# A hybrid decoder step: query and key chunks of the second mixer as pairs through memory, heads and page attention behind fourteen whole gates

## The chip, the cores and the metric

The kernel runs on one core of a Trainium2 chip. The time is the device time of one execution in microseconds (us), as the median of several runs. Engines are named as the profile names them: PE (TensorE, matmuls), PEld (its weight loads), DVE (VectorE), ACT (ScalarE), POOL (GpSimd) and SP (SyncE, which issues loads).

## The reference

One layer of a hybrid decoder, on 512 prompt tokens and 8 single decode tokens together (N = 520 columns, model width 2048). Cut to what matters:

```
sh1, sc1, g1, sh2, sc2, g2 = ada_mod(c, w_ada, b_ada)          # silu(c) @ w_ada + b_ada, six parts
h = modulate(rmsnorm(x, norm1_w), sh1, sc1)
mq, mk, mv, mo, mi, mf, fq, fk, fv, ff, ga, gb = split(h @ w_in + b_in)
y_m = mlstm(mq, mk, mv, mi, mf, mo)                            # first mixer, 4 heads
q_f = rmsnorm(split_heads(fq, 8), f_qnorm_w)
k_f = rmsnorm(split_heads(fk, 8), f_knorm_w)
y_f = fox(q_f, k_f, v_f, log_sigmoid(ff))                      # second mixer, 8 heads
merged = sigmoid(ga) * (y_m @ w_proj_a) + sigmoid(gb) * (y_f @ w_proj_b)
x = x + g1 * (merged @ w_out)
h2 = modulate(rmsnorm(x, norm2_w), sh2, sc2)
x = x + g2 * conv_ffn(h2, ...)
```

For the prompt, `fox` is causal attention with a forgetting bias. For each of the 8 decode tokens it attends to two pages of 128 cached keys and values, which a page table names, and to the token itself.

## The kernel before

All activations are stored with features on the 128 partitions and the 520 tokens along the free axis. A weight matrix is cut into *chunks* of 128 output features: a chunk of `w_in` is 128 x 2048 numbers, 1 MB. Products are made in a split precision: weights and activations are each divided into a high and a low part (`wh`, `wl` and so on; ACT casts the high part, DVE subtracts for the low one), and high x high, high x low and low x high are added in PSUM.

There are two ways to compute chunks.

- *Dense* (`dense`): for each of 16 k-blocks (K = 2048 in blocks of 128), three products for each of two halves of the tokens (260 columns): 96 matmuls. Half a chunk of weights (128 x 1024) is loaded by SP (`wraw`, a pool of 8 tiles named `raw`) and split (`wtwo`). Between k-blocks `dense` calls `step()`, which runs one entry of the list `bg`; twice a chunk it calls `due()`, which may run an entry of `pending`, by a pattern in `calls`. One k-block is called a *step* here; other work is put at steps by number.
- *In pairs* (`Pair`, `run_pairs`): two chunks are computed together with Strassen's scheme in seven products of half size, each 8 k-blocks x 3 matmuls of 260 columns (168 matmuls for two chunks). The sums of activations that this needs (`hX`) are made once; sums of weights (`sw`) are made by DVE for every pair. `run_pairs` counts in products, seven a pair; `late` maps such a number to a function that runs there. Inside it PE, DVE and ACT keep the order in which the program lists their instructions.

Everywhere else a scheduler orders instructions by their place in the program and a cost model. Loads of weights have priority and leave as soon as a tile is free.

The stages around the change, in order:

1. First mixer with dense chunks, then a few dense gates `ga` while its last heads finish (NG = 2 gates).
2. `w_pa`: 16 dense chunks of `y_m @ w_proj_a`; the conditioning part G1 rides on it as `pending` work.
3. *Pairs*: `GatePair` for the other gates `ga` (2 to 15) and for the first NB2 = 8 gates `gb`, and `ValuePair` for the values of the second mixer, which go to memory (`dv`). Sigmoids of these `gb` gates go to memory as `dsg`.
4. *Attention stage*: for each of the 8 heads a dense chunk of queries and one of keys (`f_proj`, tile `fi`), then the 8 other gates `gb` dense (`w_gate`, tile `gate`). Between their k-blocks run the heads (`f_norm_q`, `f_norm_k`, `f_scores`, `f_turn`, `f_attend`: root mean square norms, scores, softmax, transposes, products with values) and the page attention of the decode tokens (`s_rows`, `s_load` with gathers of key pages by POOL into `kp`, `s_scores` on DVE, `s_softmax`, `s_gather` with gathers of value pages into `vp`, `s_attend` on PE, `s_heads`). All this is placed by `at(chunk, k, ...)`: a head starts every two chunks, 32 steps; page scores run from the eighth head on, then every 6 steps; the first value gathers come while key gathers still run. The conditioning parts SC2 and SH2 are `pending` work here.
5. `w_pb`: 16 dense chunks of `y_f @ w_proj_b`, each multiplied by its gate `mg[j]` and added to the part from memory (`dmg`); then `w_out` in pairs, and the feed-forward part.

A conditioning part (`ada_steps`) is 16 k-blocks of a 32-column product with 2048 columns of `w_ada` (two loads of 0.5 MB a k-block), done as 8 parts of two k-blocks, and a last entry that transposes the result and adds the bias.

## Time and profile before

| | |
|---|---|
| median of 3 runs | 2865.99 us (2864.04 to 2866.9) |
| span of the profiled execution, first to last instruction | 2875.7 us |
| mean granted TensorE clock in it | 0.996 |
| PE busy | 2845.9 us (99%) |
| DVE, ACT, POOL busy | 2165.4 (75%), 1379.1 (48%), 363.6 us (13%) |
| chain that ended last, by engine | PE 89%, issue 4%, DVE 3%, DMA 2%, ACT 2% |
| moved by DMA | 514.23 MB, mean 179 GB/s |

The profiled execution has no time of its own apart from its span, which is 9.7 us above the median of the timed runs. A row of a window view gives the stretch, its length, busy time and number of instructions of PE, PEld, DVE, ACT and POOL, the granted clock, the busy share of the DMA engines and what they moved. A row of the chain of waits gives start, length, what ran, and how many instructions were merged. A row of a group gives line, engine, operation, output <- inputs, shape, count, busy time, mean length of one in ns, and the idle time before.

### The profile page before, as it was taken

Reading aid. Unit: us, or ns where it says so; the run is one execution under the profiler, and the core shown is the slowest. Engines: PE = TensorE matmul, PEld = TensorE weight load, DVE = VectorE, ACT = ScalarE, POOL = GpSimd, SP = SyncE. Lnnn points to the kernel's source line nnn. Section 1 sums busy time; section 2 is a strip of 40 time slices with the busy share of each in tenths; the row PEclk is TensorE's granted clock in tenths of the full one; section 3 lists DMA queues with packets and bytes.
Section 4 is the critical chain, followed back from the end, with each engine's and each line's share of the span. In section 5 each row is a group of like instructions: output and inputs, shape, how many; then the busy total and the mean of one; then the engine's idle time right before and its main releaser. Section 6 shows DMA issues by size and latency. Waiting matters only on the chain.

```text
span 2875.7 us, 58597 instructions
## 1 busy us (share of the span) xinstructions
PE 2845.9 (99%) x23462; PEld 2734.9 (95%) x23462; DVE 2165.4 (75%) x4016; ACT 1379.1 (48%) x2451; POOL 363.6 (13%) x649
## 2 busy tenths in 40 slices
PE   8999999999999999999999999999999999999999
PEld 6899998999998989799999999999999999999999
DVE  5987754677855667368888888888888887787787
ACT  4346643455544554335555544444444445544543
POOL 0001101221101123302111000000000001100100
PEclk9999999999999999999999999999999999999999
DMA  9934458745456676657763444444443437746752
GB/s 340 313 130 142 141 164 300 246 151 170 148 166 222 208 243 231 209 186 230 221 202 104 128 137 144 144 138 151 135 152 114 149 111 201 191 153 186 204 159 89
DMA packets 214298, 514.23 MB, mean 179 GB/s; under 512 B 24512, under 2 KB 77232, under 8 KB 214024
## 3 DMA queue, kind: packets, MB, share of 16 engines
q1 hardware_dynamic: 177232, 416.07, 44.8%
q0 software_dynamic: 36352, 94.18, 10.9%
q8 instruction: 184, 3.01, 0.4%
q14 instruction: 90, 0.74, 0.1%
q10 hardware_dynamic: 440, 0.23, 0.0%
HBM read 440.47 MB, written 66.46 MB: 176 GB/s over the span
## 4 chain that ended last, share of the span: by engine, by line
PE 89%; issue 4%; DVE 3%; DMA 2%; ACT 2%; POOL 0%; SPq 0%; ACTq 0%; POOLq 0%; DVEq 0%
PE x L60 31%; PE y L60 16%; PE z L60 8%; PE fi L221 7%; PE gate L221 4%; PE fo L60 3%; PE pa L221 3%; PE pre L60 3%; PE mo L221 2%; PE adp L417 2%; PE mv L221 2%; PE adp L60 1%; DMA ar<-in_w_ada 1%; PE mq L221 1%; PE mk L221 1%
## 5 line engine op out<-in xcount | busy, mean ns | idle before, releaser
L60 ACT CAST wh<-sw 128x512 fp32r<-128x512 f32 x638 | 365.7, 621 | 246.2 <-PE z L60 74.2
L60 DVE TENSOR_TENSOR wl<-sw,wh 128x512 fp32r<-128x512 f32 x638 | 411.2, 686 | 86.8 <-ACT wh L60 83.9
L60 PE MATMUL x<-bf,wh 128*128 128x260 f32 x2624 | 475.9, 282 | 0.2 <-DVE tg L60 0.2
L60 ACT CAST wh<-raw 128x1024 fp32r<-128x1024 f32 (+2 forms) x350 | 316.7, 917 | 296.3 <-PE x L60 132.8
L60 DVE TENSOR_TENSOR wl<-raw,wh 128x1024 fp32r<-128x1024 f32 (+2 forms) x350 | 365.8, 1056 | 123.0 <-ACT wh L60 110.5
L60 PEld LDWEIGHTS x<-bf,wh 128*128 128x128 f32 x2624 | 403.4, 188 | 0.4 <-issue 0.4
L60 PE MATMUL x<-bf,wl 128*128 128x260 f32 x1312 | 369.8, 282 | 0.0
L176 DVE TENSOR_TENSOR wl<-raw,wh 128x1024 fp32r<-128x1024 f32 (+1 forms) x115 | 139.5, 1213 | 192.4 <-ACT wh L175 178.9
L60 PEld LDWEIGHTS x<-bf,wl 128*128 128x128 f32 x1312 | 246.9, 188 | 0.0
L60 PE MATMUL y<-bf,wh 128*128 128x260 f32 x1312 | 239.3, 283 | 0.0
L175 ACT CAST wh<-raw 128x1024 fp32r<-128x1024 f32 (+1 forms) x115 | 119.5, 1040 | 216.1 <-issue 42.9
L60 DVE TENSOR_TENSOR sw<-raw,raw 128x512 f32<-128x512 f32 x316 | 203.1, 683 | 0.0
L60 PEld LDWEIGHTS y<-bf,wh 128*128 128x128 f32 x1312 | 201.9, 188 | 0.0
L60 PE MATMUL x<-ff,wh 128*128 128x260 f32 x1024 | 186.5, 283 | 0.0
L60 PE MATMUL y<-bf,wl 128*128 128x260 f32 x656 | 185.1, 282 | 0.0
L60 PEld LDWEIGHTS x<-ff,wh 128*128 128x128 f32 x1024 | 157.8, 188 | 0.0
L60 PE MATMUL x<-ff,wl 128*128 128x260 f32 x512 | 144.6, 282 | 0.0
L60 PE MATMUL x<-hf,wh 128*128 128x260 f32 x720 | 131.4, 283 | 0.0
L60 PE MATMUL fo<-fe,wh 128*128 128x260 f32 x768 | 125.6, 284 | 1.6 <-DVE fo L60 1.1
L60 PEld LDWEIGHTS y<-bf,wl 128*128 128x128 f32 x656 | 123.4, 188 | 0.0
L60 PE MATMUL z<-bf,wh 128*128 128x260 f32 x656 | 120.3, 284 | 0.0
L60 PEld LDWEIGHTS x<-hf,wh 128*128 128x128 f32 x720 | 110.7, 188 | 0.0
(641 smaller groups left out, 7586.9 us busy)
## 6 DMA issues: line engine op xcount, KB each, us to landing
raw<-in_w_fi SPq DMA_DIRECT2D x176, 512.0 KB
raw<-in_w_in SPq DMA_DIRECT2D x155, 512.0 KB
ar<-in_w_ada SPq DMA_DIRECT2D x192, 256.0 KB
raw<-in_w_ada SPq DMA_DIRECT2D x96, 512.0 KB
raw<-in_w_fo SPq DMA_DIRECT2D x64, 512.0 KB
raw<-in_w_out SPq DMA_DIRECT2D x32, 512.0 KB
raw<-in_w_fo SPq DMA_DIRECT2D x32, 384.0 KB
dff<-cc POOLq DMA_DIRECT2D x44, 260.0 KB
```

Of the source, the lines that this page charges most:

```text
L60: return lambda *a, **k: self.tc.keep_in_program_order(getattr(self.eng, op)(*a, **k))
L175: S.copy(wh[:, o], t[:, :m])
L176: V.tensor_tensor(wl[:, o], t[:, :m], wh[:, o].bitcast(F32), op=ALU.subtract)
L221: T.matmul(acc[:, z, :HN], a[:, o], b[:, z * HN:(z + 1) * HN], start=(k == 0 and i == 0), stop=(k == K - 1 and i == 2))
L417: ins = T.matmul(ps[32 * g:32 * g + 32, :], cs[:, k, :], w, start=first, stop=last, tile_position=(0, 32 * g))
```

## The change

- *Queries and keys as pairs.* A new `QueryPair` computes the query and key chunk of one head as a pair and stores both in memory (`dqk`). Eight of them follow the four value pairs. `f_proj` goes; `f_load` fetches queries, keys and values of a head from memory by SP.
- *Fewer gates as pairs.* NB2 goes from 8 to 2: six gates `gb` more become dense, 14 in all. Their chunks are stored without sigmoid (`dsg`), and `put_gate` applies it in the `w_pb` loop, where all 16 gates are now fetched, four chunks ahead.
- *SC2 among the pairs.* The part moves from `pending` into `late_steps`: from the third pair on, each pair has one k-block's loads at its product 2 and the matmuls at product 5; the transpose comes in the last pair.
- *Decode rows.* The queries and keys of the 8 decode tokens are read from `dqk` for all heads at once and normed before the attention stage, instead of being copied head by head.
- *A new plan for the attention stage.* It is written in steps (`put`): a head every 24 steps, page scores every 9 steps from step 12, value gathers from step 164, `s_attend` every 6 steps from 174. SH2 is asked for in the pattern `0, 3, 8`, three calls of `due()` in eight.

The diff, cut to its core:

```diff
+        return [on(part, k) for k in range(0, KC, 2)] + [lambda: ada_store(which, box[1])]
...
-    NB2 = 8
+    NB2 = 2
     assert (NG + NB2) % 2 == 0
-    dsg = dram([NB2, P, N], "dsg")
+    dsg = dram([KC, P, N], "dsg")
...
+    dqk = dram([2, FH, P, N], "dqk")
+
+    class QueryPair(ValuePair):
+        def __init__(self, hh):
+            self.hh = hh
+            self.chunks = [25 + 3 * hh, 25 + 3 * hh + 1]
+            Pair.__init__(self, [I["w_in"][i] for i in self.chunks], hX, ORDER, 1)
+
+        def out(self, e):
+            parts = (self.tt[:, :HN], self.tg[:, :HN]) if e == 0 else (self.tg[:, HN:N], self.tt[:, HN:N])
+            for z, t in enumerate(parts):
+                G.dma_start(dqk[e, self.hh][:, z * HN:(z + 1) * HN], t)
+
     gates = list(range(NG, KC + NB2))
     units = [GatePair(gates[2 * i:2 * i + 2]) for i in range(len(gates) // 2)]
-    units[2:2] = [ValuePair((2 * i, 2 * i + 1)) for i in range(FH // 2)]
+    units[2:2] = [ValuePair((2 * i, 2 * i + 1)) for i in range(FH // 2)] + [QueryPair(hh) for hh in range(FH)]
+    late_ada = {}
+
+    def late_load(k):
+        late_ada[k] = [wraw(I["w_ada"][k * P:(k + 1) * P, SC2 * DM + e * 1024:SC2 * DM + (e + 1) * 1024])
+                       for e in range(2)]
+
+    def late_product(k):
+        if k == 0:
+            late_ada["ps"] = mm_ps("adp")
+        raw = late_ada.pop(k)
+        ada_mm(late_ada["ps"], [(k, raw[g // 2][:, g % 2 * 512:(g % 2 + 1) * 512], k == 0, k == KC - 1)
+                                for g in range(4)], False)
+        if k == KC - 1:
+            late_ada["sb"] = ada_out(late_ada.pop("ps"), 4)
+
+    def late_turn():
+        ada_store(SC2, late_ada.pop("sb"))
+
+    late_steps = {7 * (len(units) - 1) + 2: late_turn}
+    for k in range(KC):
+        late_steps.update({7 * (2 + k) + 2: on(late_load, k), 7 * (2 + k) + 5: on(late_product, k)})
...
-    run_pairs(units, 1, {}, 0)
+    run_pairs(units, 1, late_steps, 0)
...
+    rows = pt("rows")
+    for e in range(2):
+        nc.sync.dma_start(rows[:, e * 64:(e + 1) * 64].rearrange("p (h n) -> p h n", h=FH),
+                          dqk[e, :, :, SEQ:N].rearrange("h p n -> p h n"))
+    sq = pt("sq")
+    S.activation(sq[:, :128], rows[:, :128], AF.Square)
+    psb = mm_ps("sms")
+    T.matmul(psb[:, :128], ones, sq[:, :128], start=True, stop=True)
+    sq = rsqrt([(psb[:, :128], 0, 128)], 1.0 / DK, pt("rq"))
+    V.tensor_tensor(rows[:, :128], rows[:, :128], sq[:, :128], op=ALU.mult)
+    for t, e, c, f in ((qS, 0, C_QN, DK ** -0.5), (kS, 1, C_KN, 1.0)):
+        for g in range(2):
+            o = e * 64 + g * 32
+            V.tensor_scalar(t[:, g].rearrange("p b h -> p h b"), rows[:, o:o + 32].rearrange("p (h b) -> p h b", h=4),
+                            col(c), f, op0=ALU.mult, op1=ALU.mult)
+    rows = sq = t = None
...
-    def f_proj(H, i):
-        wi[0] = 25 + 3 * H.i + i
-        acc, t, n = w_in("fi")
-        S.activation(z2(t), acc, AF.Identity, bias=col(C_BIN + n - 1))
-        return t
-
-    pending += ada_steps(SC2) + ada_steps(SH2)
-    calls[:] = 0, 1, 2
+    def f_load(H):
+        H.q, H.k, H.v = (st("fi") for _ in range(3))
+        for t, src in ((H.q, dqk[0]), (H.k, dqk[1]), (H.v, dv)):
+            nc.sync.dma_start(t[:, :N], src[H.i])
+
+    pending += ada_steps(SH2)
+    calls[:] = 0, 3, 8
...
-    def at(chunk, k, f, *a):
-        plan.setdefault(chunk * KC + k, []).append(on(f, *a))
-
+    def put(s, f, *a):
+        plan.setdefault(s, []).append(on(f, *a))
+
+    HP = 24
     heads = []
     for hh in range(FH):
         H = Head()
         H.i, H.p, H.pt = hh, [], {}
         heads.append(H)
-        c = 2 * hh
-        at(c + 1, 6, f_norm_q, H)
-        at(c + 2, 5, f_norm_k, H)
-        at(c + 2, 7, f_forget, H)
-        at(c + 2, 9, f_values, H)
-        at(c + 2, 14, f_scores, H, 0)
-        at(c + 2, 14, f_scores, H, 1)
-        at(c + 3, 0, f_scores, H, 2)
-        at(c + 3, 2, f_scores, H, 3)
-        for k, j in ((8, 0), (9, 1), (10, 2)):
-            at(c + 3, k, f_turn, H, j)
+        b = 8 + hh * HP
+        if hh:
+            put(b - 12, f_load, H)
+        put(b - 3, lambda H=H: f_square(H, H.q))
+        put(b + 3, f_norm_q, H)
+        put(b + 4, lambda H=H: f_square(H, H.k))
+        put(b + 9, f_norm_k, H)
+        put(b + 11, f_forget, H)
+        put(b + 13, f_values, H)
+        for s, i in ((17, 0), (17, 1), (19, 2), (21, 3)):
+            put(b + s, f_scores, H, i)
+        for j in range(3):
+            put(b + 28 + j, f_turn, H, j)
         for j in range(NB):
-            at(c + 3, 12 + j, f_attend, H, j)
-    for e, c in enumerate((7, 15)):
-        at(c, 12, s_rows, e)
-        for i in range(1 + e):
-            at(c + 1, 2 + 9 * i, s_load, e * 8 + i)
-    for i in range(8):
-        at(8 + i, 11 if i % 2 == 0 else 4, s_scores, i)
-        if i < 7:
-            at(8 + i, 14 if i % 2 == 0 else 7, s_load, i + 1)
-        at(16, 12 + 6 * i, s_scores, 8 + i)
-        if i < 6:
-            at(16, 15 + 6 * i, s_load, 10 + i)
-    for i in range(8):
-        at(18, 12 + i, s_gather, i)
-    at(19, 8, s_bias)
-    at(19, 11, s_softmax)
-    at(20, 2, s_weights)
+            put(b + 34 + j, f_attend, H, j)
+    f_load(heads[0])
+    for e in range(2):
+        put(1 + e, s_rows, e)
+    s0, ds = 12, 9
+    for i in range(16):
+        put(s0 + ds * i - (8 if i else 4), s_load, i)
+        put(s0 + ds * i, s_scores, i)
+    put(154, s_bias)
+    put(155, s_softmax)
+    put(162, s_weights)
+    for i in range(4):
+        put(164 + i, s_gather, i)
     for n in range(8):
-        at(20, 6 + 7 * n, s_attend, n)
-        for i in range(n * 4 + 8, min(n * 4 + 12, 32)):
-            at(20, 6 + 7 * n + 1 + i % 4, s_gather, i)
+        t = 174 + 6 * n
+        put(t, s_attend, n)
+        for i in range(n * 4 + 4, min(n * 4 + 8, 32)):
+            put(t - 5 + i % 4, s_gather, i)
         if n % 2:
-            at(20, 6 + 7 * n + 3, s_heads, n // 2)
+            put(t + 3, s_heads, n // 2)
 
     def y_split(hh):
         yf[hh] = split(sp, "s", yf[hh], "yf", SEQ)
 
     for hh in range(FH):
-        at(19, 14 + 7 * hh, y_split, hh)
+        put(max(182 + 4 * hh, 8 + hh * HP + 39), y_split, hh)
...
-    for H in heads:
-        H.v = st("fi")
-        nc.sync.dma_start(H.v[:, :N], dv[H.i])
-        H.q = f_proj(H, 0)
-        f_square(H, H.q)
-        H.k = f_proj(H, 1)
-        f_square(H, H.k)
     H = None
     mg = [None] * KC
-    calls[:] = 0, 0, 1
 
     def fetch_gate(j):
         mg[j] = st("sgm")
         nc.sync.dma_start(mg[j][:, :N], dsg[j])
 
+    def put_gate(j):
+        if j >= NB2:
+            S.activation(mg[j][:, :N], mg[j][:, :N], AF.Sigmoid)
+
     for j in range(NB2, KC):
-        if j == NB2 + 3:
-            calls[:] = 0, 1, 5
-        mg[j] = w_gate(j, 1)
+        i = 1 + 24 + 24 + KC + j
+        acc = dense(I["w_in"][i], h, "gate")
+        t = st("sgm")
+        S.activation(z2(t), acc, AF.Identity, bias=col(C_BIN + i - 1))
+        G.dma_start(dsg[j], t[:, :N])
+    t = None
     flush()
-    fetch_gate(0)
-    fetch_gate(1)
+    order = [j for i in range(8) for j in (i, 8 + i)]
+    for j in order[:4]:
+        fetch_gate(j)
...
-        if n % 2 == 0 and n // 2 + 2 < NB2:
-            fetch_gate(n // 2 + 2)
+        if n + 4 < KC:
+            fetch_gate(order[n + 4])
+        put_gate(j)
```

More of the change, by code (lines that the diff above doesn't have):

```diff
@@ L517, in part, with ada_store @@
                 box.append(ada_out(box[0], 4))
-        def last():
-            t = ada_turn(box[1], 4)
-            c0 = which * 16
-            dst = ada[:, c0:c0 + 16, :].rearrange("p (g j) i -> p j g i", g=4)
-            bias = wide(C_ADA + c0, 16).rearrange("p (g j) i -> p j g i", g=4)
-            for j in range(4):
-                V.tensor_tensor(dst[:, j], t[:, j, :, :9], bias[:, j], op=ALU.add)
-            if which == SC2:
-                ada_add_one(c0, 16, C_N2)
-        return [on(part, k) for k in range(0, KC, 2)] + [last]
+        return [on(part, k) for k in range(0, KC, 2)] + [lambda: ada_store(which, box[1])]
+    def ada_store(which, sb):
+        t = ada_turn(sb, 4)
+        c0 = which * 16
+        dst = ada[:, c0:c0 + 16, :].rearrange("p (g j) i -> p j g i", g=4)
+        bias = wide(C_ADA + c0, 16).rearrange("p (g j) i -> p j g i", g=4)
+        for j in range(4):
+            V.tensor_tensor(dst[:, j], t[:, j, :, :9], bias[:, j], op=ALU.add)
+        if which == SC2:
+            ada_add_one(c0, 16, C_N2)
     SH1, SC1, G1, SH2, SC2, G2 = range(6)
@@ L1439, in f_norm_k @@
         G.dma_start(O["kT"][:, H.i, :], H.k[:, :N])
-        V.tensor_copy(kS[:, H.i // 4, :, H.i % 4], H.k[:, SEQ:N])
         H.kr = split(sp, "s", H.k, "fk", SEQ, G if H.i < FH - 1 else V)
@@ L1446, in f_norm_q @@
         f_norm(H.q, qwc, H)
-        V.tensor_copy(qS[:, H.i // 4, :, H.i % 4], H.q[:, SEQ:N])
         H.qr = split(sp, "s", H.q, "fq", SEQ, G)
@@ L1862, in tile_hybrid_step @@
     units = [WoPair(c) for c in range(0, KC, 2)]
-    order = [j for i in range(8) for j in (i, 8 + i)]
     early = {}
```

## The prediction

> **What bounds the kernel now.** I read the page's busy shares first, then the stages around the change, then the chain for the price of one matmul, then the places where TensorE loses time.
>
> ```profile
> span 2875.7 us, 58597 instructions
> PE 2845.9 (99%) x23462; PEld 2734.9 (95%) x23462; DVE 2165.4 (75%) x4016; ACT 1379.1 (48%) x2451; POOL 363.6 (13%) x649
> ```
>
> TensorE (PE) is busy in all but 30 us. Busy time can hide a loss, though: a stretch shown below is busy throughout with a quarter fewer matmuls, so I count matmuls. Next the stages, whose columns are PE, weight loads, DVE, ACT, POOL (time and instructions), clock, DMA share, GB/s: the pairs, the attention stage (16 query/key chunks, then 8 gates), and the `w_pb` stage.
>
> ```profile
> 536.00:837.00 301.00, 301.00 (x2521) 301.00 (x2520) 233.27 (x398) 156.79 (x311) 44.95 (x85) 1.00 0.50 165
> 837.00:1229.70 392.70, 387.77 (x3065) 343.75 (x3064) 210.97 (x472) 177.28 (x330) 92.37 (x92) 0.99 0.66 220
> 1229.70:1325.00 95.30, 95.30 (x796) 95.25 (x795) 72.61 (x120) 36.46 (x55) 13.35 (x25) 1.00 0.65 203
> ```
>
> The pairs have no idle PE time at 77% DVE. In the chain of waits (start, length, what, matmuls) the same product returns every pair, the same point of a head every two chunks, and a conditioning part (`adp`) has a piece of its own.
>
> ```profile
> 439.42 11.65 PE pa L221 x96
> 452.92 11.65 PE pa L221 x96
> 519.00 17.18 PE pa L221 x144
> 553.40 5.74 PE x L60 x48
> ...
> 814.44 5.74 PE x L60 x48
> 911.03 3.62 PE fi L221 x30
> 945.04 3.62 PE fi L221 x30
> 1657.35 3.12 PE adp L60 x16
> ```
>
> From 553.40 to 814.44 are 13 pairs: 20.08 us each. A pair is 7 products of 8 x 3 matmuls, 168: 119.5 ns a matmul. A dense chunk is 16 x 3 x 2 = 96 matmuls; 17.18 us for 144 is 119.3 ns, the same. Dense or paired, a matmul costs the same; two chunks are 192 of them dense and 168 as a pair. The matmul count is the bound.
>
> **The change part by part.**
>
> *Chunks that change sides.* Two gates came before (NG = 2): the pairs were 22 gates and 8 values, 15 units (301.0 us / 20.08); they become 16 gates, 8 values, 16 queries and keys, 20 units. The dense gates go from 8 to 14, the dense query/key chunks from 16 to none. Out: 16 x 96 - 8 x 168 = 192 matmuls. Back in: 6 x 96 - 3 x 168 = 72. Net 120 matmuls x 119.5 ns = **-14.3 us**, all on the engine that sets the end. The work around the pairs (ACT, DVE and POOL ends of a query pair: those of a value pair, with half its stores) goes where DVE has 23% free: nothing.
>
> *The SC2 part among pairs.* Its matmuls stay the same; only their grouping changes.
>
> ```profile
> 858.91 1.85 PE adp L417 x16
> ```
>
> Eight blocks of 16 (1.85 us; the `pa` rows stand 13.50 apart, 11.65 + 1.85) become 16 blocks of 8. A block's own cost beyond its matmuls is what a chunk with one loses: 11.65 - 96 x 0.1195 = 0.18 us. Eight blocks more: +1.4 us. From below 0; from above the 3.12 us block, an `adp` inside pairs: 8 x (3.12 - 1.85) + 1.4 = +11.6. I take **+1.4**, since most parts inside pairs and all those before are 1.85 and the loads come three products (8.6 us) ahead. Weight tiles: six of eight slots per unit instead of four. On SP's queue today a pair's loads leave in one group, a pair apart:
>
> ```profile
> 706.59 6.80 SPq L161 DMA_DIRECT2D raw<-in_w_in  x4
> 726.72 6.76 SPq L161 DMA_DIRECT2D raw<-in_w_in  x4
> ```
>
> By the order of release (two slots after the third product, one after the fifth, three after the sixth) every load still leaves at least three products before its use. A pair then moves 3 MB in 21 us, 150 GB/s, beside stores: nothing.
>
> *The rows of the decode queries and keys.* Two small loads, one 128-column matmul, a root and six small DVE steps before the attention stage: +0.5 us on PE, bounded by 0 and by the wait for a load that comes late, some 3 us (`adp` above, 3.12 - 1.85, doubled). `vS`, a load of the same kind, left at 663.3, far ahead of its stage, so I take the low side.
>
> ```profile
> L1418 SPq DMA_DIRECT2D vS<-dv x1: 377/377/377, 663.3 to 663.3; - x1
> ```
>
> *The attention stage.* Heads now come every 24 steps (a step is one k of a dense chunk) instead of 32, page scores every 9 steps from the first head on. Does another engine become the bound? Head periods without and with two page scores, then a pair stretch:
>
> ```profile
> 911.00:945.00 34.00, 34.00 (x276) 30.06 (x274) 17.93 (x43) 17.20 (x34) 3.17 (x3) 1.00 0.61 201
> 1011.80:1045.80 34.00, 34.00 (x275) 30.08 (x275) 21.96 (x51) 17.15 (x34) 7.06 (x7) 1.00 0.76 246
> 1344.00:1404.00 60.00, 60.00 (x504) 60.00 (x503) 51.17 (x98) 34.66 (x58) 11.69 (x18) 1.00 0.69 211
> ```
>
> ```profile
> L176 DVE TENSOR_TENSOR wl<-raw,wh 128x1024 fp32r<-128x1024 f32 x48 | 58.8, 1224 | 118.3 <-ACT wh L175 105.2 <-issue 5.5 <-PE nFb L408 3.5
> ```
>
> A head's own PE work is 34.0 - 192 x 0.1195 - 2 x 1.85 = 7.4 us. A new period is 24 x 6 x 0.1195 + 7.4 + 0.86 x 1.85 = 26.2 us of PE. DVE in it: head 17.93 - 4 x 1.224 = 13.0, three splits 3.7, 2.67 page scores at (21.96 - 17.93) / 2 = 2.0 each 5.4; together 22.1 us, 84%. The last row has DVE at 85% with 504 matmuls in 60.00 us, 119 ns: not slowed. ACT is at 62% by the same sum, POOL lower. I take nothing for it; bounds 0 and 10% of the stage. The evictions of the 14 gates replace those of 16 chunks; their sigmoid moves to `w_pb`, and all 16 gates are now fetched there, four chunks (23 us) ahead:
>
> ```profile
> L1231 ACT ACTIVATE sgm<-gate,sv 128x520 f32<-128x520 f32 x7 | 4.9, 693 | 0.6 <-remote 0.4 <-PE gate L221 0.2
> ```
>
> 14 x 0.69 = 10 us beside ACT's 36.46 of 95.30 us: hidden by the dense matmuls; behind a late gate the weight casts would queue, one chunk ahead of PE. The seam to `w_pb` has 5 steps after the last page head instead of 6:
>
> ```profile
> 1226.72 0.50 DVE L1697 TENSOR_TENSOR yfl<-yS,yfh 128x8 fp32r<-128x8 f32 x4
> ```
>
> This ends 2.5 us before `w_pb` begins at 1229.7; a step less (0.72 us) leaves 1.8. The loads of queries and keys add two transfers per head on SP's queue, where weights stand behind them; eight weight slots cover that. The stores of the gates go to POOL's queue ahead of page gathers: 14 issues, covered because a gather is wanted only 8 steps later.
>
> *Bytes.* The stage moved 392.7 us x 220 GB/s = 86 MB. Less 10 chunks (10.5 MB) and SC2 (16.8), plus queries, keys (4.3) and gate stores (3.4): 66 MB. Length: 392.7 - 10 x 11.47 - 8 x 1.85 - stalls = 250 to 263 us; 250 to 265 GB/s.
>
> *The stalls that exist.* PE loses time near the end of the stage without waiting for a semaphore:
>
> ```profile
> PE gate L221 <- issue: 4.0, 9, 0.7
> ```
>
> ```profile
> 994.00:1002.00 8.00, 8.00 (x66) 7.87 (x65) 5.13 (x10) 3.57 (x8) 3.26 (x3) 1.00 1.01 354
> 1140.00:1148.00 8.00, 7.53 (x56) 6.74 (x54) 5.50 (x8) 0.00 (x0) 6.48 (x6) 1.00 0.90 295
> 1148.00:1156.00 8.00, 5.86 (x28) 4.37 (x28) 4.94 (x8) 1.74 (x2) 5.49 (x6) 0.85 0.71 225
> 1156.00:1164.00 8.00, 8.00 (x49) 7.79 (x50) 2.31 (x5) 2.33 (x2) 0.00 (x0) 0.73 0.41 144
> 1188.00:1196.00 8.00, 7.43 (x58) 6.10 (x57) 1.23 (x1) 1.64 (x2) 2.30 (x3) 1.00 1.02 389
> 1204.00:1212.00 8.00, 6.87 (x51) 5.51 (x52) 1.23 (x1) 1.64 (x2) 2.08 (x3) 1.00 0.51 173
> ```
>
> Against 66 matmuls in 8 us (first row) the next three miss 10 + 38 + 17 = 65, 7.8 us, and the last two 8 + 15, 2.8 us: 10.6 us in all. By busy time they would be 0.5 + 2.1 + 0.0 + 0.6 + 1.1 = 4.3 us, and the stall terms below a gain of 0.6 us instead of 5.8; the 1156 row, fully busy with 49, decides for counts. The Trainium skill (Perfetto Trace Analysis, Identifying the Most-Contended Engine) says the same, that matmul occupancy is no good measure since pipelined matmuls overlap. In that row the clock is 0.73. What stands beside the stalls is POOL's queue, in trains of gathers:
>
> ```profile
> 1136.86 0.95 POOL L877 DMA_INDIRECT vp<-in_cache_v,idx  x1 [0.30 <-issue]
> ...
> 1154.06 0.95 POOL L877 DMA_INDIRECT vp<-in_cache_v,idx  x1 [0.30 <-issue]
> 1188.93 0.95 POOL L877 DMA_INDIRECT vp<-in_cache_v,idx  x1 [0.30 <-issue]
> ```
>
> The long stall starts half-way in a train of 14, in which key gathers (every 6 steps) and the first 8 value gathers run together; the short ones end trains of 8. In the new plan the last key load is at step 139 and the first value gather at step 164, so the train of 14 goes: -7.8. The value gathers keep their trains (4 per 6 steps, 4 per 7 now): 2.8 stays. In exchange SH2's parts come in two bursts of three, 15 weight tiles of 0.5 MB in three calls (28 us) beside 4.9 MB of other loads: 12.7 MB, of which 4 MB can lie ready, at the 295 to 389 GB/s of the rows 22 to 30 us. Within 2 us each of just enough: **+2** for both, bounds 0 and 8. Sum of the stalls: **-5.8**.
>
> *Sum.* -14.3 + 1.4 + 0.5 - 5.8 = -18.2 us. It is made against the profiled execution, whose span, 2875.7, is 9.7 us above the median of the runs, 2865.99; the stages are a few per cent of it, so I subtract from the median: 2847.8, **2848 us**.
>
> **The rivals.**
>
> *The stalls only move.* Gathers, gates and parts stand denser, and PE loses about what it lost (10.6 us): -14.3 + 1.9 = 2853.6 us. For it: 220 GB/s become some 260. Against it: the 994 row, 1.01 and 354 GB/s with 66 matmuls.
>
> *The denser attention stage starves PE (slower).* Place: the two bursts (56 us) and the value gathers (50 us). At the rate of 1140 to 1156 (84 of 132 matmuls, 36% lost) that is 38 us, of which 10.6 are there already: 2865.99 - 12.4 + 27 = 2881. It decides from a loss of 12.4 + 10.6 + 5.7 = 28.7 us, 80 us of such stretches. For it: today's stall came at only 225 to 295 GB/s. Against: that took POOL's longest train. The Trainium skill (Runtime: NRT & Kernel Launch, Instruction fetch mechanics) says that an engine's instructions come by DMA too, and that this is mostly hidden; if these are late instructions, more bytes mean more of them, and by that page alone the price would be near none. No row here tells it apart.
>
> *DVE becomes the bound there.* At 84% its queue delays the splits of the weights; half of the 10% bound, 5% of 252 us: 2848 + 13 = 2861. Against: the 85% row.
>
> *The parts among pairs wait for their tiles.* Slots too few; each of 16 products waits 2 us, a load's landing after a late release: 2848 + 32 = 2880. Against: the release order above.
>
> **How the numbers follow.** Forecast 0.50 (own range 2841 to 2853), moved stalls 0.25, starved PE 0.12, DVE 0.08, tiles 0.05. The low end is -12.4 with all stalls and the extra 1.4 gone, -10.6 - 1.4: 2841, set at 2839; the high end leaves out 0.17 and reaches past the DVE case: 2864. A change under 0.2% (5.7 us) can't be told from none: faster 0.50 + 0.25 + 0.03, same 0.08, slower 0.14.
>
> **What would show it.** The pairs last 20 x 20.08 + 17 = 418 us without idle PE; the attention stage 250 to 256; DVE near 84% in its middle; no 8 us with under 50 matmuls; `w_pb` still 119 to 120 ns a matmul. Wrong if `x`, `y`, `z` of the pairs stand more than 119.5 ns apart, if PE waits for DVE's `wl` or for a `raw` load, or if several windows lose a third of their matmuls.

## The result, and the profile after

The changed kernel takes 2909.35 us (median of 4 runs, 2906.55 to 2911.15), the kernel before 2865.6 us (4 runs, 2864.04 to 2866.9): ratio 1.015, 95% interval 1.0136 to 1.0165. It is 44 us slower, where 18 us faster was forecast. The profiled execution has a span of 2909.5 us, which is typical of its runs.

The window view of the changed kernel, in the same three stages and columns as before: pairs, attention stage, `w_pb`.

```profile
538.00:959.60 421.60, 421.60 (x3495) 405.91 (x3494) 309.56 (x528) 209.46 (x418) 55.69 (x105) 1.00 0.57 190
959.60:1264.40 304.80, 271.68 (x1972) 225.48 (x1971) 190.73 (x440) 146.62 (x298) 102.36 (x105) 0.96 0.64 216
1264.40:1356.00 91.60, 91.60 (x767) 91.60 (x766) 68.08 (x113) 43.30 (x68) 11.76 (x22) 1.00 0.71 224
```

The first and the last row are as forecast: no idle PE time, 421.6 us against 418, and 119.4 ns a matmul in `w_pb`. The loss is in the middle row. It was to last 250 to 256 us; it lasts 305, with PE idle for 33 us and the granted clock at 0.96. Its bytes are as counted ahead: 304.8 us at 216 GB/s are 65.8 MB, against 66. Its worst stretch, ten microseconds to a row:

```profile
1020.00:1030.00 10.00, 8.50 (x68) 7.92 (x70) 7.26 (x12) 3.52 (x6) 2.56 (x3) 1.00 0.98 314
1030.00:1040.00 10.00, 5.02 (x36) 1.29 (x35) 5.60 (x10) 3.80 (x7) 1.45 (x2) 1.00 0.91 315
1040.00:1050.00 10.00, 2.73 (x6) 0.38 (x8) 0.00 (x0) 0.00 (x0) 2.57 (x3) 0.51 0.99 372
1050.00:1060.00 10.00, 10.00 (x56) 6.57 (x53) 4.74 (x22) 4.82 (x13) 0.00 (x0) 0.81 0.38 129
```

From 1040 to 1050 almost nothing computes (PE starts 6 matmuls) and the DMA engines are full (0.99, 372 GB/s). The chain of waits says what is awaited:

```profile
970.06 1.85 PE adp L417 x16
...
1032.32 2.77 PE adp L417 x22
...
1035.37 0.54 SPq L161
...
1036.00 13.15 DMA raw<-in_w_ada
1049.15 0.04 issue
1049.19 1.92 PE adp L417 x4
...
1067.27 8.90 DMA fi<-dqk
...
1107.22 4.90 DMA raw<-in_w_ada
1112.16 4.45 PE adp L417 x12
```

A part of SH2 (16 matmuls) that stands alone takes its 1.85 us, like the one at 970.06. By the plan its eight parts come 0, 48, 336, 384, 432, 720, 768 and 816 dense matmuls into the stage. In the trace, counted in PE's order, the scheduler has put parts 4 and 5 and 10 matmuls of part 6 together at 384, with no dense matmul between them, and the other 38 at 672. A weight tile serves 4 of these matmuls, so 42 need 11 tiles, and the pool has 8 slots. The tiles of part 6 could be asked for only from 1035.37 on, when the products before it had given slots free, and the one that the chain names takes 13.15 us to land. PE keeps its order and waits. The 42 matmuls take 22.4 us from start to next start and the 38 take 11.4, where 1.85 us for every 16 would be 4.9 and 4.4.

In the 1050 row the clock is at 0.81 although PE has work again. The Trainium skill (TensorE: Matmul & The Clock Gate, Part 1: The HAM clock gate) says that the clock is halved after an idle window of some 3.4 us and returns after a busy one: the 0.51, and then 0.81 with 56 matmuls, agree. An idle stretch is thus paid a second time, here with some 2 us (0.19 of the 1050 row).

The waits of PE's matmuls in the stage (us, times, longest) name next the end of a head's chain on VectorE, GpSimd and ScalarE:

```profile
PE adp L417 <- DMA raw<-in_w_ada: 14.5, 4, 11.6
PE ms L394 <- DVE fpl L233: 6.9, 2, 5.9
PE fS L1203 <- POOL fkl L233: 4.1, 3, 2.1
PE fS L1203 <- ACT last L1511: 2.6, 2, 1.4
```

### The profile page after: what moved, and what is told of

Its sections match the earlier page's. It is cut to its first block, busy times and chain, and to the rows that moved or that the text cites. A ratio compares the mean times of both kernels' runs of the same rounds, so it can differ in the third digit from the quotient of the medians.

```text
span 2909.5 us, 58777 instructions
## 1 busy us (share of the span) xinstructions
PE 2849.6 (98%) x23344; PEld 2721.3 (94%) x23344; DVE 2221.6 (76%) x4114; ACT 1409.4 (48%) x2541; POOL 385.0 (13%) x683
## 4 chain that ended last, share of the span: by engine, by line
PE 85%; issue 5%; DMA 4%; DVE 4%; ACT 2%; POOL 1%; SPq 0%; POOLq 0%; ACTq 0%; DVEq 0%
PE x L60 33%; PE y L60 17%; PE z L60 8%; PE gate L221 4%; PE fo L60 3%; PE pre L60 3%; PE pa L221 3%; PE mo L221 2%; PE adp L60 2%; PE mv L221 2%; PE adp L417 1%; DMA ar<-in_w_ada 1%; DMA fi<-dqk 1%; PE mq L221 1%; PE mk L221 1%
## 5 line engine op out<-in xcount | busy, mean ns | idle before, releaser
L60 DVE TENSOR_TENSOR wl<-sw,wh 128x512 fp32r<-128x512 f32 x678 | 436.9, 685 | 96.1 <-ACT wh L60 93.3
L60 ACT CAST wh<-sw 128x512 fp32r<-128x512 f32 x678 | 388.6, 621 | 245.3 <-PE z L60 74.7
L60 ACT CAST wh<-raw 128x1024 fp32r<-128x1024 f32 (+2 forms) x380 | 333.7, 893 | 337.3 <-PE x L60 142.7
L60 DVE TENSOR_TENSOR wl<-raw,wh 128x1024 fp32r<-128x1024 f32 (+2 forms) x380 | 385.2, 1027 | 122.8 <-ACT wh L60 107.8
L60 DVE TENSOR_TENSOR sw<-raw,raw 128x512 f32<-128x512 f32 x336 | 215.9, 683 | 1.3 <-DMA tot<-sq 1.2
L176 DVE TENSOR_TENSOR wl<-raw,wh 128x1024 fp32r<-128x1024 f32 (+1 forms) x95 | 115.0, 1211 | 113.0 <-ACT wh L175 106.8
L60 PE MATMUL x<-hf,wh 128*128 128x260 f32 x960 | 175.5, 283 | 0.0
L175 ACT CAST wh<-raw 128x1024 fp32r<-128x1024 f32 (+1 forms) x95 | 98.5, 1038 | 154.4 <-PE gate L221 44.6
L60 PEld LDWEIGHTS x<-hf,wh 128*128 128x128 f32 x960 | 147.8, 188 | 0.0
L60 PE MATMUL x<-hf,wl 128*128 128x260 f32 x480 | 135.1, 282 | 0.0
```

Of the source, the lines that this page charges most:

```text
L60: return lambda *a, **k: self.tc.keep_in_program_order(getattr(self.eng, op)(*a, **k))
L175: S.copy(wh[:, o], t[:, :m])
L176: V.tensor_tensor(wl[:, o], t[:, :m], wh[:, o].bitcast(F32), op=ALU.subtract)
```

## The experiments

The kernel before, run beside them, took between 2863.4 and 2879.2 us from chip to chip; so stages of profiled executions are compared. "Stage" is the time from the last pair matmul to the first `w_pb` matmul, and the products' columns are the sums over the stage of the time from a matmul's start to the next matmul's, both worked out from the trace. `sO` are the page sums, `fS` the heads' scores. "Together" is the largest number of `adp` matmuls that stand in PE's order with no dense matmul between them; the scheduler orders everything anew after each edit, so this changes even where the plan of SH2 doesn't. Each row is one execution.

| kernel | pairs | stage | adp | together | dense, ns a matmul | fS | sO | time of one run |
|---|---|---|---|---|---|---|---|---|
| before, its second profile (e10) | 301.1 | 381.2 | 29.7 | 16 | 125 | 16.4 | 8.0 | 2865.1 |
| before, SC2 among pairs (e9) | 321.0 | 373.1 | 14.8 | 16 | 128 | 17.0 | 8.0 | 2876.2 |
| changed | 421.5 | 304.9 | 40.3 | 42 | 138 | 24.4 | 13.0 | 2911.2 |
| SH2's parts spread (e1) | 421.5 | 307.4 | 40.4 | 50 | 132 | 30.7 | 17.0 | 2912.6 |
| heads' loads 8 steps earlier (e2) | 421.5 | 319.6 | 42.9 | 64 | 138 | 20.4 | 14.2 | 2924.0 |
| SH2 without its loads (e4) | 421.5 | 279.0 | 20.0 | 16 | 134 | 19.8 | 15.8 | 2886.5 |
| key pages loaded once (e5) | 421.5 | 293.3 | 31.6 | 42 | 133 | 26.7 | 13.8 | 2897.9 |
| heads' loads by GpSimd (e12) | 421.5 | 300.4 | 20.3 | 32 | 141 | 29.2 | 14.4 | 2904.9 |
| relaxed plan, 16 gates (e7) | 401.4 | 336.6 | 34.8 | 48 | 141 | 23.7 | 19.0 | 2921.7 |
| SH2 among pairs too (e6) | 441.3 | 265.9 | - | - | 134 | 26.2 | 14.0 | 2892.0 |
| e6 with the relaxed plan (e8) | 421.2 | 293.8 | - | - | 137 | 19.4 | 22.9 | 2897.8 |
| e6, longer chains (e11) | 441.3 | 271.4 | - | - | 142 | 20.9 | 15.9 | 2896.4 |
| e6 without page scores (e13) | 441.3 | 246.4 | - | - | 128 | 20.0 | 14.6 | 2871.2 |
| e6, scores without gathers (e14) | 441.3 | 254.5 | - | - | 131 | 23.6 | 12.7 | 2876.5 |
| e6, gathers without scores (e15) | 441.3 | 249.2 | - | - | 131 | 20.2 | 14.1 | 2875.6 |
| e6, value pages earlier (e17) | 441.3 | 264.3 | - | - | 133 | 24.7 | 14.7 | 2890.0 |
| changed, no SH2 loads, no scores (e16) | 421.5 | 264.6 | 16.6 | 16 | 128 | 18.7 | 16.4 | 2871.0 |

**e10: the kernel before, profiled again.** No edit.

> The kernel before, unchanged, for a second profile of it. The prediction took 10.6 us of stalls near the end of its attention stage from one profiled execution whose span is 9.7 us above the median of the runs. Theory G (that profile was an odd one): the long stall at 1140 to 1156 and the low granted clock behind it are not there again, the stage lasts 384 to 388 us in place of 392.6 and the span is near 2864 us; then the prediction subtracted 5.8 us that a typical execution does not lose. Rival: the stall is there again, stage 391 to 394 us, and the step stands.

The span is 2863.3 us and the stage 381.2, 11.4 us shorter than in the first profile and shorter than the 384 expected at least. The rows of the stretch that held the long stall:

```profile
1140.00:1148.00 8.00, 8.00 (x69) 8.00 (x69) 5.33 (x9) 2.65 (x3) 6.36 (x6) 1.00 0.81 272
1148.00:1156.00 8.00, 6.99 (x58) 6.52 (x56) 6.75 (x12) 1.05 (x1) 5.72 (x6) 1.00 0.85 281
1156.00:1164.00 8.00, 8.00 (x66) 7.78 (x66) 4.89 (x11) 6.31 (x9) 1.49 (x3) 1.00 0.52 171
```

The first profile had 28 and 49 matmuls in the last two, at clocks 0.85 and 0.73; here are 58 and 66, at 1.00. Theory G holds: the stall belonged to that execution. From here on this profile is the one compared with. A dense matmul of the old stage takes 125 ns from start to start and its conditioning part of 128 matmuls 14.8 us. The forecast's own rule, ten chunks and SC2 less, applied to this profile gives 381.2 - 960 x 0.125 - 14.8 = 246.4 us: the changed stage is 58.5 us over that. By product: adp +25.5 (40.3 - 14.8), dense matmuls +17, fS +8, sO +5, the rest 3.

**e9: SC2 among pairs, alone.** In the kernel before, the SC2 parts go into units 2 to 9, two to a unit, and off `pending`.

```diff
...
-    run_pairs(units, 1, {}, 0)
+    run_pairs(units, 1, late_steps, 0)
...
-    pending += ada_steps(SC2) + ada_steps(SH2)
+    pending += ada_steps(SH2)
```

> The kernel before with one part of the change alone: SC2's product among the pairs (two parts to a unit in units 2 to 9), everything else as it was. Pairs 301.1 + 16 x 1.22 = 321 us, attention stage 392.6 less the same 19.5 = 373 us, run level with the kernel before within 3 us if a part costs the same in both places. Theory D: the loads that it takes out of the stage save some more, attention 362 to 370 us, run 3 to 10 us faster. If that part of the change is itself at fault, the run is over 5 us slower.

The pairs rise by 19.9 us, 1.24 a k-block (8 matmuls); adp in the stage falls by 14.8, and the stage by 8.1 in all, since its dense matmuls take 128 ns in place of 125. The expectation took 1.22 us a k-block for the dense stage too, where a block of 16 costs 1.85, 0.93 a k-block. In the chain of the changed kernel a block of 8 matmuls and the `z` product behind it, and a `z` without one:

```profile
572.51 2.86 PE z L60 x24
...
592.59 0.99 PE adp L60 x8
593.58 3.08 PE z L60 x24
```

The small block costs 0.99 and sets the next product back by 0.22. The grouping alone costs 5 us, not 1.4, and no load that it takes out of the stage pays for it there. The run is 10 us slower than the kernel before on its chip, which the expectation took as the sign that this part of the change is itself at fault; one execution each doesn't say how much of the other 5 us is chance.

**e1 and e2: SH2's bursts, the heads' loads.** e1 spreads the parts, e2 asks for the heads' loads earlier.

```diff
-    calls[:] = 0, 3, 8
+    calls[:] = 0, 1, 3
```

> The changed kernel with SH2's nine entries asked for in every third call (0, 1, 3) instead of three calls in eight; same work, same bytes. Theory A (bursts): three parts in a row want 12 tiles of 0.5 MB beside the dense weights, and PE stands at adp for 18.3 us in the changed kernel's trace (1034 to 1049 and 1104 to 1112) with what follows from it; spread, that goes: 2909 falls by 20 to 30 us, to 2880 to 2890, and no adp waits over 1 us for its tile. Theory B (the heads' queries and keys arrive late by themselves) or C (DVE stands behind page gathers): the waits at adp go, but PE then waits elsewhere, and the time falls by under 10 us, above 2899.

```diff
-            put(b - 12, f_load, H)
+            put(b - 20, f_load, H)
```

> The changed kernel with a head's loads of queries, keys and values placed 20 steps before its base step instead of 12 (8 steps, some 8 us, earlier). Theory B: ACT stands 15.6 us in five waits at the squares for these loads, DVE and PE behind it; earlier loads take these away and 12 to 20 us with them: 2889 to 2897. Theory A: the weights' bursts fill the queue whatever stands in it, the change is within 6 us of 2909. Earlier loads could also take tiles that others need, and then it is slower.

e1 takes the same 40.4 us of adp and the stage is no shorter, but it doesn't refute the bursts, because they are still there. The scheduler left parts 1 to 4 alone and put the next 50 matmuls together: the four take 1.9 to 3.8 us each, the 50 take 27.3. Earlier loads of the heads lengthen the stage by 15 us, so theory B falls; here 64 matmuls stand together, and they take 34.2 us.

**e4 and e5: loads left out.** e4 multiplies one tile 32 times over; e5 gathers the first score's key pages, and its query row, for all.

```diff
-            raw = [[wraw(I["w_ada"][i * P:(i + 1) * P, ...]) for e in range(2)] for i in (k, k + 1)]
...
+            raw = [[one_raw[0]] * 2] * 2
...
```

> The changed kernel with all matmuls of SH2 but only one tile of its weights loaded and used again (SH2's values are left out): 16 MB less traffic in the attention stage, PE's work as before. If the stage is short of DMA (A, or bytes in general) it comes near the forecast, 2850 to 2862. If its queues and plan are too tight by themselves (B, C) it stays above 2880.

```diff
+        if i:
+            W.k[i] = W.k[0]
+            return
...
```

> The changed kernel with the key page loads and gathers of the first page score only; the other 15 use the same tiles (their scores are left out), so DVE does all its page work and waits for no page. Theory C: the wait of 6 us at 1131, where DVE stands at a page product and PE behind it, goes, with smaller ones: -8 to -15 us, 2894 to 2901. It also takes 12 MB of traffic away, so by the shortage of DMA alone it falls by more, 15 to 25 us. Under theory B alone it changes by less than 5 us.

Without SH2's loads the stage is 25.9 us shorter and adp takes 20.0; the run, 2886.5 us, stays above 2880, which the expectation took as the sign that queues and plan are too tight by themselves. Without the later gathers it is 11.6 us, of which adp is 8.7. That run lies in theory C's range, but not by C's mechanism, VectorE's wait for pages: most of the gain is at SH2's tiles. Neither stage comes to 246.

**e12: another queue for the heads' loads.**

```diff
-            nc.sync.dma_start(t[:, :N], src[H.i])
+            G.dma_start(t[:, :N], src[H.i])
```

> The changed kernel with one edit: the loads of a head's queries, keys and values are issued on GpSimd's queue in place of SyncE's, so weight tiles no longer stand behind them there. Theory J (the order in SyncE's queue: a load that waits for its slot holds up the weight tiles behind it): the waits of adp for its tiles (18 us) fall by half or more, stage 304.9 to 290 us or less, run near 2895 us. Theory D (too many bytes in too short a stage): the waits stay, stage 300 to 310 us. A third: the heads' loads now hold up page gathers on GpSimd's queue, and the stage gets longer, over 310 us.

adp falls to 20.3 us, as without loads, and PE's matmuls no longer wait for `raw`. Theory J foretold that, but its mechanism is not what took the longest wait away. The tiles of part 6 are asked for at nearly the same time, the first 75.8 us after the start of the stage in the changed kernel and 75.6 in e12, the last 89.0 and 88.0. Two rows of SyncE's issues, first of the changed kernel, then of e12:

```profile
1035.37 3.36 SPq L161 DMA_DIRECT2D raw<-in_w_ada  x3
...
1048.56 0.33 SPq L161 DMA_DIRECT2D raw<-in_w_ada  x1
```

```profile
1033.38 2.80 SPq L161 DMA_DIRECT2D raw<-in_w_ada  x3
...
1045.79 0.33 SPq L161 DMA_DIRECT2D raw<-in_w_ada  x1
```

What differs is PE's order. In e12 the scheduler put 32 matmuls at 384 and part 6 a whole chunk later, at 480, and PE works while its tiles come, with the DMA engines at 0.89:

```profile
1040.00:1050.00 10.00, 10.00 (x85) 9.86 (x84) 5.07 (x11) 4.34 (x8) 0.59 (x1) 1.00 0.89 351
```

This agrees with the column "together": 42 matmuls or more cost 20 to 34 us at that one place, 32 cost 6 (e12), and 16 cost 1.9 to 3.8. A run that changes SH2's place in PE's order and nothing else was not made.

The stage gains only 4.5 us. Among its first waits (PE's weight loads; us, times, longest) are now:

```profile
PEld fS L1203 <- ACT last L1511: 7.6, 4, 3.2
...
PEld fPT L1543 <- DVE rt L1484: 4.1, 2, 3.9
```

Now the heads' chains are late. Whether they are so by themselves, or because their loads now stand in GpSimd's queue, this run doesn't tell.

**e6, e7, e8: SH2 among pairs, and a relaxed plan.** e6 puts both conditioning products among the pairs, two parts a unit; e7 stretches the changed kernel's plan over 16 whole gates; e8 does both.

```diff
...
+    for n, w in enumerate((SC2, SH2)):
+        for k in range(KC):
+            b = 7 * (2 + 8 * n + k // 2) + 3 * (k % 2)
+            late_at(b + 2, late_load, w, k)
+            late_at(b + 5, late_product, w, k)
...
-    pending += ada_steps(SH2)
```

> SH2's product is moved among the pairs too (SC2's parts two to a unit in units 2 to 9, SH2's two to a unit in 10 to 17), so the stage behind the pairs holds no conditioning load at all and the result stays whole. Theory D (the stage asks for more bytes than come in time, through one queue that serves its loads in order): the stage falls from 304.9 us to about 260 us, which is what it had without SH2's loads (279.0) less SH2's own matmuls (16 parts of 1.22 us), the pairs rise from 421.5 to 441 us, and the run ends near 2884 us, 25 us under the changed kernel. Theory E (each head's chain of VectorE, ScalarE and GpSimd steps has too few k-steps of cover, 24 where it had 32, whatever is loaded): SH2's product goes with its 19.5 us, its waits turn into others, the stage stays near 285 us and the run near 2909 us. A third, F: the pairs, which now load four weight tiles more a unit, lose more than 1.22 us a part (pairs over 450 us).

```diff
-    NB2 = 2
+    NB2 = 0
...
-    HP = 24
+    HP = 28
...
-    s0, ds = 12, 9
+    s0, ds = 12, 11
...
```

> All 16 gates are whole behind the pairs (one pair unit fewer), and the plan is stretched over their 256 k-steps: 28 steps a head in place of 24, 11 a score in place of 9, the values' part 30 steps later. Without any effect of density the pairs lose 21 us (400), the stage gains two chunks of 96 matmuls at 119.5 ns (23 us: 328) and the run ends 2 us slower than the changed kernel, 2911 us. Theory E: the stage's lost time, some 50 us beyond its matmuls, falls by half or more, stage 300 us, run near 2885 us. Theory D: the same bytes over a stage longer by an eighth lose a third less, stage 310 to 315 us, run near 2896 us.

> Both together: SH2 among the pairs, 16 whole gates, the plan over 256 steps. Theory D alone: what SH2's loads cost is gone already, so the stage is 260 plus two chunks (23) = 283 us, the pairs 420 us, the run near 2886 us, no better than with SH2 among the pairs alone. Theory E: the heads' chains have room, the stage goes to 265 us or less and the run to about 2868 us, level with the kernel before.

e6: the stage falls to 265.9, six above theory D, the pairs to 441.3 as foretold. The run is 19 us better than the changed kernel, and still behind the one before. More steps for a head gain nothing: e7 is 32 us longer than the changed stage, 8 more than its two chunks (192 matmuls at 125 ns, 24 us); e8 is 28 longer than e6's, 4 more than its two. Theory E falls, at least as a matter of how far apart the heads stand.

**e11, e13: a longer chain, no page scores.** Both on e6. e11 moves a head's values and forget row to its start and makes its scores and what follows three steps later; e13 drops the page scores.

```diff
-        put(b + 11, f_forget, H)
-        put(b + 13, f_values, H)
-        for s, i in ((17, 0), (17, 1), (19, 2), (21, 3)):
+        put(b + 1, f_forget, H)
+        put(b + 2, f_values, H)
+        for s, i in ((20, 0), (20, 1), (22, 2), (24, 3)):
...
```

> On the kernel with both conditioning products among the pairs, whose attention stage of 265.9 us still holds some 18 us of waits of TensorE, mostly for the last steps of a head's chain: each head's forget row and values are transposed right at its start (steps 1 and 2 in place of 11 and 13) and its scores, turns and sums come three steps later, so that the chain behind the keys' norm has 11 steps in place of 8 and two fewer evictions in it. Theory H (the plan's distances inside a head are too short): the waits for fk, last and nfb go, stage 250 to 256 us, run near 2878 us. Theory I (the waits come from the page scores that stand in VectorE's and GpSimd's queues between a head's steps): no change beyond 4 us, stage 262 to 268 us.

> On the kernel with both conditioning products among the pairs: the page scores are left out (no key gathers, no copies of the query rows, none of their VectorE work; the page part of the softmax then works on zeros). Theory I: most of the 18 us of waits go, stage 245 to 250 us, run near 2872 us. Theory H: the waits inside a head's chain stay, stage 260 us or more.

e11 is 5.5 us longer, outside the ranges of both theories: H falls. e13 is 246.4, at the low end of theory I: 19.5 us of the stage come from the page scores, though e13 drops no dense matmul. Windows of 30 us in the middle of e6, then of e13 (PE, weight loads, VectorE, ScalarE, GpSimd):

```profile
1009.00:1039.00 30.00, 28.58 (x228) 27.46 (x227) 26.30 (x57) 16.87 (x34) 11.77 (x11) 1.00 0.65 211
1069.00:1099.00 30.00, 26.20 (x195) 23.98 (x194) 23.58 (x45) 15.77 (x31) 8.47 (x8) 0.98 0.52 154
1099.00:1129.00 30.00, 25.38 (x182) 24.10 (x180) 23.00 (x52) 13.00 (x27) 9.53 (x10) 0.91 0.54 178
```

```profile
1068.00:1098.00 30.00, 29.93 (x235) 28.70 (x234) 19.00 (x46) 20.04 (x42) 6.07 (x6) 1.00 0.40 125
1098.00:1128.00 30.00, 29.95 (x243) 29.00 (x242) 19.56 (x45) 19.18 (x38) 5.82 (x6) 1.00 0.38 126
```

In these rows, with VectorE at 77 to 88% PE does 182 to 228 matmuls a window, with VectorE at 63 to 65% it does 235 to 243. The share alone doesn't order them: 88% has the 228, 77% the 182. e6's DMA share, 0.52 to 0.65, leaves room.

One more thing stands in these traces. The 32 products of the page scores take VectorE 28.7 us in the changed kernel and 22.0 in the one before. The middle one is as long as before, but seven take over 1 us, and each of these overlaps a subtraction on GpSimd for the low part of a head's queries or keys. The group before (from e10) and after, then one of the seven with the subtraction beside it:

```profile
L60 DVE TENSOR_TENSOR kp<-kp,qb x32: 674/683/751, 982.8 to 1153.9; 128x512 f32<-128x512 f32 x32
L60 DVE TENSOR_TENSOR kp<-kp,qb x32: 671/684/2665, 987.6 to 1182.3; 128x512 f32<-128x512 f32 x32
...
995.95 1.87 DVE L60 TENSOR_TENSOR kp<-kp,qb 128x512 f32<-128x512 f32 x1
...
995.97 1.30 POOL L233 TENSOR_TENSOR fkl<-fi,fkh 128x512 fp32r<-128x512 f32 x1
```

In six of the seven, length less overlap is 0.55 to 0.58 us by the profile's spans, as if VectorE stood still meanwhile. In e10 no such overlap is longer than 0.2 us. (In the kernel before the scores start in the ninth chunk, with the fifth head, not with the eighth.) What this costs the stage was not tried.

**e14, e15: which half of the page scores.** e14 keeps VectorE's work and drops all gathers and query rows but the first (e5's edit, on e6); e15 keeps the loads and drops the VectorE work.

```diff
...
-            v.tensor_tensor(kp[:, :512], kp[:, :512], qb[:, :512], op=ALU.mult)
-            v.tensor_reduce(sc[:, g, b, e * 4:e * 4 + 4], ..., axis=AX.X, op=ALU.add)
```

> On the kernel with both conditioning products among the pairs (stage 265.9 us; 246.4 us with the page scores left out altogether): the key pages and the query row are loaded for the first score only, and all 16 scores do their VectorE work on those tiles. Theory V (VectorE's time is what the scores cost: 43 us more of it in this stage, in order with every step of a head): nearly all of the 20 us stays, stage 261 to 267 us. Theory P (GpSimd's queue: gathers that wait for a tile hold up the low parts of the keys behind them; with the bytes of the gathers): stage 246 to 252 us. Both halves: in between.

> The other half, on the same kernel: all 32 key pages are gathered and all query rows loaded, but the scores' multiplications and sums on VectorE are left out. Theory V: stage 246 to 250 us. Theory P: 258 us or more.

VectorE's work alone costs 8.1 us over e13, the gathers alone 2.8, both 19.5. e15 lies in theory V's range and e14 between the two, so neither theory is right by itself: VectorE's half is the larger, and 8.6 us arise only where the two meet. These are single executions, each with an order of its own. One way in which they meet is in GpSimd's waits in e6's stage (us, times, longest): a gather stands first in its queue until VectorE or another engine frees a tile, and the low parts of the queries and keys stand behind it.

```profile
POOL kp L877 <- DVE lo L386: 27.2, 4, 13.3
...
POOL kp L877 <- DVE sm L1540: 9.8, 2, 8.2
```

Whether this is the whole of the 8.6 us was not tried.

**e16: both causes out of the changed kernel.** e4's and e13's edits together.

> The changed kernel with SH2's loads left out (one weight tile serves all of its products) and the page scores left out. If the loss of the attention stage is these two and nothing else of size, it is what the stage without scores and without SH2 had (246.4 us) plus SH2's matmuls in blocks of 16 at 1.85 us (14.8): 259 to 264 us, the pairs at 421.5, the run near 2864 us. If a third cause is left that moving SH2 had hidden, the stage is over 268 us.

The stage is 264.6 us, between the two ranges of the expectation, and the run 2871.0 where 2864 was expected. The stage has 259.74 us of PE and a clock of 1.00:

```profile
958.50:1223.10 264.60, 259.74 (x1973) 222.62 (x1972) 146.86 (x376) 145.78 (x297) 67.39 (x73) 1.00 0.44 139
```

So 40 of the 58.5 us go with SH2's loads and the page scores: 26 with the loads alone (e4), 14 more here. SH2's parts stand apart in this run, as planned. Of the 18 left, 8.4 are in sO, 4 in the dense matmuls, 2 each in fS and adp.

**e17: value pages earlier.** On e6.

```diff
-            put(t - 5 + i % 4, s_gather, i)
+            put(t - 10 + i % 4, s_gather, i)
```

> On the kernel with both conditioning products among the pairs: the value pages are gathered 4 to 5 steps earlier. In the changed kernels the four products of a group of page sums often start one behind the other (some 450 to 520 ns apart) as their pages land one by one, where the kernel before starts all four within 20 ns; its 64 products take 8.0 us there and 14.0 here. If lateness of the pages does that, they fall to 8 to 10 us and the stage to 259 to 262 us. If the groups are torn apart by something else (VectorE, PSUM), they stay at 13 to 14 us and the stage at 264 to 268 us.

sO stays at 14.7 us and the stage at 264.3. That doesn't clear the late pages. The gathers start 4.5 us earlier than in e6, but the scheduler put the sums earlier too (first at 1187.8 us, 1190.4 in e6), and they wait more for landings: their weight loads 4.5 us, 2.7 in e6. In the trace the four products of a group start 7 ns apart where the group is whole; where it is torn, most gaps are 0.33 to 0.45 us and some 0.9 to 2.5. At three of the gaps matmuls of the heads stand between in PE's order. What tears the rest stays open.

## Why the prediction was wrong

- *Counts.* Held, and better: ten dense chunks were 120 us in the stage (125 ns a matmul, not the 119.5 of `w_pa` and the pairs), five more pairs 100.4: -19.6 instead of -14.3.
- *SC2 among pairs, +1.4.* The mechanism was there, the size was not: +5 (e9). The 0.18 us of a block was taken from blocks of 16 inside dense chunks; among pairs the eight blocks more cost 5.1 us, 0.64 each. The upper bound, 11.6, held it.
- *Decode rows, +0.5.* Their matmuls take 0.4 us in the stage; held within what can be seen.
- *The attention stage, "I take nothing for it", bounds 0 and 10% of the stage.* This step failed: without adp the stage lost 33 us (dense matmuls 17, fS 8, sO 5, the rest 3), more than its upper bound of 25. The 85% row that excluded VectorE came from the pairs of `w_out` behind `w_pb`, where 43 of VectorE's 51 us are sums and splits of weights. In the attention stage its work is links of chains that go PE, ScalarE, VectorE, GpSimd and back to PE, and there 77 to 88% went with a loss of a twentieth to a quarter of the matmuls (e6 against e13). The page scores are 14 (e16) to 19.5 us (e13) of the loss, by VectorE's work and the gathers together.
- *SH2's bursts, +2, bounds 0 and 8.* This step failed too: adp took 25.5 us more than 14.8. The sum gave a burst 28 us of dense work in which its bytes could come, and the bytes were right. In the trace the scheduler had left no dense work between most of three parts, and eight slots hold the tiles of two. "Eight weight slots cover that", said of the heads' loads, isn't shown wrong: without them in SyncE's queue the tiles of the longest wait were asked for at most 1 us sooner (e12).
- *Stalls, -5.8.* There was next to nothing to remove: the long stall isn't in the second profile (e10), and the first one's span, 9.7 us above the median, was the sign of it. The sum should not have taken a gain from rows of an execution that is slower than the runs and then subtracted it from their median.
- *Page gathers covered by 8 steps.* Their sums took 13.0 us instead of 8.0; cause open (e17).
- *Seam and `w_pb`.* Held, 91.9 us in both; gates and sigmoids are hidden there.
- *Rivals.* "The denser attention stage starves PE" had the sign and, with the bursts, the place, at 2881 us and a chance of 0.12. Its price came from the stall of the odd execution, and the value gathers at the end, its other place, are not the main loss. "DVE becomes the bound there" named the other half, and sized it as delayed weight splits at 13 us. Each was priced as if the other were absent. "The parts among pairs wait for their tiles" didn't come: the pairs have no idle PE time. Two of the prediction's own signs of being wrong did: PE waits for a `raw` load, and rows lose a third of their matmuls and more.

The terms between the forecast of 2848 and 2909: +8 for the stall of the odd execution (the -7.8 in the -5.8), +4 for SC2, -5 for the counts, +56 for the stage (58.5 less the 2 for the bursts and 0.5 for the decode rows that were in the sum already). Together 63 us, by single profiled executions, against 61 by the medians.

No version here beats the kernel before. Even without page scores (e13) or without those and SH2's loads (e16) the run takes 2871 us.

## What to carry to other kernels

Taking dense work out of a stage takes away the cover of everything else that stage does: list what is left per us of it on each engine and each queue, and don't call an engine free at 85% because another stage runs at 85%; ask whether its work is ahead of PE or a link in a chain that comes back to PE. Where a scheduler orders the work, read from the trace where it stands on the engine: parts that the plan spreads can stand together there, and an edit elsewhere can move them. Profile the kernel before twice before counting a stall in it as a gain, above all where its span lies above the median. Where two resources get tight at once, take away each alone and both together: here the halves gave 8 and 3 us and the whole 19.

## What the runs showed of the hardware

- Four matmuls on different 32-column blocks start 7 ns apart and cost 0.5 us together if they stand ready one behind the other (sO: 8.0 us for 64 in e10); in torn groups most gaps are 0.2 to 0.5 us and some over 0.8 (sO: 12.7 to 22.9 us in the changed kernels). The same holds for adp: 1.85 us for 16, and 4.45 for 12 where tiles land one by one. The Trainium skill (TensorE: Matmul & The Clock Gate, Part 3: Packing small matmuls) tells of the overlap; that a late tile costs the overlap beside the wait is from these rows.
- A PE stall of 11.6 us is followed by a row at 0.81 of the clock, so stalls cost more than their length.
- Busy DMA engines did not hold PE up where its operands were there: 85 matmuls in 10 us at 0.89 and 351 GB/s (e12), against 6 at 0.99 and 372 GB/s where PE stood at a tile (the changed kernel).
- Seven page products on VectorE took 1.1 to 2.7 us beside a subtraction on GpSimd, and none of 32 took over 0.75 us in e10.
